# A gated delta rule's query decayed on GpSimd, its output summed in PSUM, and another scheduler model

## The chip, the cores and the metric

The kernel runs on one core of one Trainium2 chip. A core has TensorE (PE, matmuls; PEld is its weight load), VectorE (DVE), ScalarE (ACT), GpSimd (POOL) and a queue that issues DMAs (SP). The time is device microseconds of one launch, as the median over runs. A profiled execution gives a span (first to last instruction) and its own time, which is a little longer.

## The reference, cut to what matters

A decoder trunk of two layers over 1024 tokens of width 1024, all in float32. Layer 0 (even) is a dilated attention and an HGRN2 recurrence side by side, layer 1 (odd) a gated delta rule. Each layer is a projection in, the mixer, a projection out. The change touches the odd layer's recurrence, and the order of instructions everywhere.

```python
# per head, in chunks; q and k normalized, g the summed log decay inside a chunk
attn_qk = einsum('bhnid,bhnjd->bhnij', qc, kc) * decay
q_dec = qc * exp(gcum)[..., None]
k_tail = kc * exp(gcum[..., -1:] - gcum)[..., None]
def step(state, inp):
    v_new = u_n - einsum('bhcd,bhdv->bhcv', w_n, state)
    o = einsum('bhcd,bhdv->bhcv', qd_n, state) + einsum('bhij,bhjv->bhiv', a_n, v_new)
    new_state = state * gl_n + einsum('bhcd,bhcv->bhdv', kt_n, v_new)
```

There are 8 key heads and 16 value heads; two value heads share a key head's q and k and differ in their decays. The output o has two parts: what the state gives to the decayed q, and what the chunk's own values give.

## The kernel before

Matmuls of the projections run as three fp32r products of a high and a low part each (`mm3`, L151 to L153), 512 columns wide. Weights are cut into these parts by ACT (L116) and DVE (L117), one unit ahead.

The odd layer works on pairs: one key head and its two value heads, hh = 0 to 7, in chunks of 128 tokens (NT = 8). Three kinds of work are interleaved:

- `proj(j)` first runs `way_out(j - 2)` (two gate projections oz and the output of a finished pair), then four projections with a short convolution: k of pair j + 1 (tile kT), two halves v of pair j, q of pair j. `conv` runs one projection as two halves of 512 tokens. ACT copies a half from its PSUM bank into a staging tile (tag ub, one buffer; the profile calls its tiles uk, uv, uq after the projection); only then the target tile is asked for (`k_tile`, `q_tile`, `v_tile`), written by ACT (L902), and three DVE operations (L904), a Tanh (L907) and one more DVE operation (L908) finish it. Projections have two PSUM banks (tag "pj").
- `invert(hh)` builds the lower triangular matrices of a pair from kT (kk, L1063), inverts them in 32x32 blocks on DVE (L1084, L1086), and joins the blocks with small matmuls (qp, up, q, u) through bank "c". Its result U lies in the tile L.
- `recur(hh)` walks the eight chunks. For each: ks = kT'S (L1182), r (L1185, DVE), qs = q'S (L1188) with the two scalings oq (L1191, ACT), vp = U r (L1197), vt (L1200, DVE) and vn (L1202, ACT), kv (L1206), the new state S (L1210, DVE), op = A vn (L1217), the sum of op and oq into bv (L1220, DVE), squares for the norm (L1225, ACT). A for the next chunk comes from `attend`: qk (L1168) times the decay tile gca, which is read by DMA from gcd, added to a mask on POOL (L1156) and put through Exp on ACT (L1158).

PSUM has tags with a number of banks each: "pj" 2, "a" 2, "b" 2, "c" 1, "d" 1. Before, ks, kv and op take "b" in turn, and qs, vp and qk share the one bank "d".

The loop over pairs mixes the three: while recur(hh) runs, the fill is proj(hh + 1) blended with invert(hh + 1). Each generator yields rough amounts of PE time, and `mix` and `blend` lay as much fill between two steps as the yielded need says; in the last pair the output projection `out_last` is fill too.

```python
fill = proj(hh + 1) if hh < 7 else seq(way_out(6), gate7(), out_last(range(3), ["pj"]))
if hh < 7:
    fill = blend(invert(hh + 1), fill, 0.8)
mix(recur(hh), fill, 2.8)
drain(fill)
```

This makes an order of emission. The framework then lays out each engine's instructions: going through a simulated run of the program, it takes on every engine the first in the order of emission that is ready in that simulation, and it gives a tile a buffer of its tag when one is free (a buffer comes free when all who read or write its tile are done). In the attention of layer 0 the order of PE (for its last pair also that of DVE) is fixed as emitted (`manual_schedule`); everywhere else the simulation decides. What an engine runs on the chip is that fixed order, each instruction waiting for its semaphores.

A tag's buffers: kT 3, q 2, kn 3, L 2, bv 2, gca 2, ub 1. At the end, `y_parts(0)` of the odd layer takes two kT buffers and two kn buffers for the first tile of the output projection's input.

Of the kernel before, what the change touches and what calls it, by code (L numbers as in the profile page):

```python
# [82 lines left out]
def trunk_kernel(ctx: ExitStack, tc: tile.TileContext, x, ew, ewo, ow, owab, owo, nw, fnw, lbl, hnw,  # L83
# [11 lines left out]
    def bank(tag, shape, name):  # L95
        return pp.tile(shape, F32, name=name, tag=tag, bufs=BANKS[tag])
# [720 lines left out]
    def odd_layer(es):  # L817
# [107 lines left out]
        def k_tile(j):  # L925
            KT[j] = sp.tile([P, T], F32, name=f"kT{j}", tag="kT", bufs=3)
            return KT[j]
# [116 lines left out]
        def invert(hh):  # L1044
# [14 lines left out]
            for h in range(2):  # L1059
# [4 lines left out]
                for c in range(4 * h, 4 * h + 4):  # L1064
# [3 lines left out]
                    for e in range(2):  # L1068
                        dve.scalar_tensor_tensor(L[:, 2 * c + e, :], kk[:, c - 4 * h, :], SC[hh][:, 0, c, e:e + 1],
                                                 gcB[:, e, :], op0=ALU.mult, op1=ALU.mult)  # L1070
                yield (15 if h else 7.0), 0.9

# [36 lines left out]
            dve.tensor_copy(Q_[a0[1], :, 0:32], qp[a0[1]])  # L1109
            yield 1.5, 1.3  # L1110
            up = bank("c", [P, 16, 32], f"up{hh}")
# [12 lines left out]

            yield 2.0, 1.8
            for h in range(2):
# [22 lines left out]
        def recur(hh):  # L1149
# [4 lines left out]
            def decay_a(c):  # L1154
                DA = decays(hh, c, "a")
                pool.tensor_tensor(DA, DA, MA[:, None, :].to_broadcast([P, 2, 128]), op=ALU.add)  # L1156
                for e in range(2):
                    act.activation(DA[:, e, :], DA[:, e, :], AF.Exp, bias=gt["ngc"][:, c, 2 * hh + e:2 * hh + e + 1])  # L1158
                return DA

            def attend(c):

                DA = ahead_a.pop()
                if c < NT - 1:
                    ahead_a.append(decay_a(c + 1))
                qk = bank("d", [P, 128], f"qk{hh}_{c}")
                s = slice(c * 128, (c + 1) * 128)
                pe.matmul(qk, kT[:, s], q[:, s], start=True, stop=True)  # L1168
                A = sp.tile([P, 2, 128], F32, name=f"A{hh}_{c}", tag="A", bufs=2)
                dve.tensor_tensor(A, qk[:, None, :].to_broadcast([P, 2, 128]), DA, op=ALU.mult)  # L1170
                return A

            ahead_a = [decay_a(0)]
            yield 1.0
            A = attend(0)
            St = None
            for c in range(NT):
                col = [slice(2 * hh + e, 2 * hh + e + 1) for e in range(2)]
                s = slice(c * 128, (c + 1) * 128)
                if c:  # L1180
# [3 lines left out]
                    for e in range(2):  # L1184
                        dve.scalar_tensor_tensor(r_[:, e, :], ks[:, e, :], SC[hh][:, 1, c, e:e + 1],  # L1185
                                                 bv[:, c, e, :], op0=ALU.mult, op1=ALU.add)
                    qs = bank("d", [P, 2, 128], f"qs{hh}_{c}")
                    pe.matmul(qs, q[:, s], St, start=True, stop=True)  # L1188
                    oq = sp.tile([P, 2, 128], F32, name=f"oq{hh}_{c}", tag="oq")
                    for e in range(2):  # L1190
                        act.activation(oq[:, e, :], qs[:, e, :], AF.Copy, scale=gt["eg"][:, c, col[e]])  # L1191
                else:
                    r_ = bv[:, 0]
                yield 1.0
                vp = bank("d", [P, 2, 128], f"vp{hh}_{c}")
                for e in range(2):
# [7 lines left out]
                if c < NT - 1:  # L1204
# [9 lines left out]
                    St = Sn  # L1214
                op = bank("b", [P, 2, 128], f"op{hh}_{c}")
                for e in range(2):
                    pe.matmul(op[:, e, :], A[:, e, :], vn[:, e, :], start=True, stop=True)  # L1217
                A = attend(c + 1) if c < NT - 1 else None
                if c:
                    dve.tensor_tensor(bv[:, c], op, oq, op=ALU.add)  # L1220
                else:
                    dve.tensor_copy(bv[:, c], op)
                for e in range(2):
# [11 lines left out]
        def y_parts(g):  # L1235
            if g:
                return *y_tile(f"lo{g % 2}", 8 + g), g * 256
            yh = [sp.tile([P, T], F32R, name=f"oyh{c}", tag="kT", bufs=3) for c in range(2)]
            yl = [sp.tile([P, T], F32R, name=f"oyl{c}", tag="kn", bufs=3) for c in range(2)]
# [109 lines left out]
```

## Time and profile before

| | |
|---|---|
| median of 3 runs | 2271.49 us (2265.71 to 2271.65) |
| profiled execution | 2270.35 us, span 2268.6 us |
| mean granted TensorE clock | 0.992 |
| PE, PEld busy | 2162.0 us (95%), 1760.6 us (78%) |
| DVE, ACT, POOL busy | 1409.7 us (62%), 950.0 us (42%), 239.5 us (11%) |
| DMA | 184.15 MB, mean 81 GB/s |

How to read what follows: the busy slices are tenths of 40 equal parts of the span. A group's row has its line, engine, operation, tiles (out<-in) and shapes, then busy us and mean ns of one, then the engine's idle time just before these and what ended most of it. A row of one tile has the durations' least, middle and largest in ns and the first and the last start in us. A row of the timeline begins with the start and the duration in us. Waits have total us, times and the longest. PE's records of matmuls overlap, so the distance between starts says what one costs.

### The profile page before, as it was taken

What the parts mean: (1) busy time and instruction counts of PE and PEld (TensorE: products, weight loads), DVE (VectorE), ACT (ScalarE), POOL (GpSimd) and SP (SyncE); (2) the same over time, 40 slices, a digit from 0 to 9 for tenths busy, and PEclk for the clock granted to TensorE, in tenths of its full rate; (3) what the DMA queues carried; (4) which work ended last, traced back from release to release, by engine and by line L of the source; (5) the groups of instructions that cost most, each with busy time, mean ns of one, the idle gap of its engine ahead of it and who ended that gap; (6) DMA issues with size and microseconds to landing.
All of it is one profiled execution on the core that took longest, in us unless ns stands there. A gap on an engine that the chain in (4) does not pass through costs nothing. (4 is left out here: it accounts for less than half of the span.)

```text
span 2268.6 us, 52553 instructions
## 1 busy us (share of the span) xinstructions
PE 2162.0 (95%) x21781; PEld 1760.6 (78%) x21781; DVE 1409.7 (62%) x3236; ACT 950.0 (42%) x2551; POOL 239.5 (11%) x252
## 2 busy tenths in 40 slices
PE   7999999999999999989999988989898999899998
PEld 6888888898877878767886776767777777678787
DVE  6353535453444344457776986968878787755767
ACT  5233333333232232222237664655555555544223
POOL 0010101010000000000000013121212121210000
PEclk9999999999999999989999999999999999999999
DMA  4111111114342334353233222121212122124233
GB/s 146 38 48 48 43 49 47 48 34 126 91 128 71 109 91 122 97 162 108 93 116 104 61 55 67 51 78 41 77 51 76 49 71 65 58 64 153 85 112 112
DMA packets 100079, 184.15 MB, mean 81 GB/s; under 512 B 12672, under 2 KB 30208, under 8 KB 99840
## 3 DMA queue, kind: packets, MB, share of 16 engines
q1 hardware_dynamic: 99840, 180.79, 25.9%
q8 instruction: 171, 2.80, 0.5%
q14 instruction: 68, 0.56, 0.1%
HBM read 151.25 MB, written 29.49 MB: 80 GB/s over the span
## 5 line engine op out<-in xcount | busy, mean ns | idle before, releaser
L117 DVE TENSOR_TENSOR w_lo<-raww,w_hi 128x512 fp32r<-128x512 f32 x292 | 210.2, 722 | 199.5 <-ACT w_hi L116 196.8
L116 ACT CAST w_hi<-raww 128x512 fp32r<-128x512 f32 x292 | 181.1, 620 | 298.0 <-DMA raww<-in_ewo_dram 51.0
L647 ACT ACTIVATE P<-P,nm 128x256 f32<-128x256 f32 (+7 forms) x128 | 71.4, 559 | 133.9 <-DVE nm L645 133.9
L151 PE MATMUL op<-w_hi,yplo 128*128 128x512 f32 x288 | 113.7, 395 | 3.3 <-DVE hr L296 1.7
L153 PE MATMUL op<-w_hi,yplo 128*128 128x512 f32 x288 | 112.2, 390 | 0.0
L152 PE MATMUL op<-w_lo,yplo 128*128 128x512 f32 x288 | 112.2, 390 | 0.0
L151 PE MATMUL oz<-hn_hi,w_hi 128*128 128x512 f32 x256 | 109.9, 429 | 0.0
L151 PE MATMUL pv<-hn_hi,w_hi 128*128 128x512 f32 x256 | 106.7, 417 | 0.5 <-ACT uv L899 0.5
L296 DVE TENSOR_TENSOR hr<-hr,op 128x512 f32<-128x512 f32 x128 | 85.9, 684 | 34.2 <-PE op L153 33.6
L153 PE MATMUL pv<-hn_hi,w_lo 128*128 128x512 f32 x256 | 104.1, 407 | 0.0
L152 PE MATMUL oz<-hn_lo,w_hi 128*128 128x512 f32 x256 | 103.0, 402 | 0.0
L153 PE MATMUL oz<-hn_hi,w_lo 128*128 128x512 f32 x256 | 102.5, 400 | 0.0
L152 PE MATMUL pv<-hn_lo,w_hi 128*128 128x512 f32 x256 | 102.2, 399 | 0.0
L653 DVE STREAM_TRANSPOSE PB<-P 128x256 f32<-128x256 f32 (+3 forms) x64 | 54.6, 853 | 72.8 <-ACT P L647 72.8
L1156 POOL TENSOR_TENSOR gca<-gca,MA 128x256 f32<-128x256 f32 x64 | 50.6, 791 | 453.8 <-DMA gca<-gcd 252.8
L296 DVE TENSOR_TENSOR hres<-hres,op 128x512 f32<-128x512 f32 x96 | 64.7, 682 | 31.8 <-PE op L153 29.4
L642 DVE CUSTOM_DVE_ANT_0 P<-S,G 128x256 f32<-128x256 f32 (+7 forms) x128 | 58.2, 492 | 36.8 <-PE S L638 35.2
L904 DVE SCALAR_TENSOR_TENSOR vT<-uv,cws,vT 128x512 f32<-128x512 f32 x96 | 74.3, 774 | 4.7 <-ACT vT L902 3.8
L1084 DVE TENSOR_TENSOR tm<-Lp,Tp 128x126 f32<-128x126 f32 (+22 forms) x248 | 74.9, 302 | 3.7
L1158 ACT ACTIVATE gca<-gca,g_ngc 128x128 f32<-128x128 f32 x128 | 45.8, 401 | 69.3 <-POOL gca L1156 69.1
L151 PE MATMUL avp<-w_hi,hn_hi 128*128 128x256 f32 x256 | 74.5, 291 | 0.0
L151 PE MATMUL op<-w_hi,yphi 128*128 128x512 f32 x160 | 65.9, 412 | 8.5 <-ACT yphi L116 4.6
(367 smaller groups left out, 6292.1 us busy)
## 6 DMA issues: line engine op xcount, KB each, us to landing
raww<-in_ew_dram SPq DMA_DIRECT2D x128, 256.0 KB, 3.0
raww<-in_ow_dram SPq DMA_DIRECT2D x100, 256.0 KB, 3.0
V<-vd SPq DMA_DIRECT2D x64, 256.0 KB, 5.3
rawy<-ymix SPq DMA_DIRECT2D x64, 256.0 KB, 2.7
raww<-in_ewo_dram SPq DMA_DIRECT2D x32, 256.0 KB, 3.0
gcl<-gcd SPq DMA_DIRECT2D x64, 128.0 KB, 3.0
gca<-gcd SPq DMA_DIRECT2D x64, 128.0 KB, 3.0
ymix<-oy SPq DMA_DIRECT2D x32, 256.0 KB, 2.0
```

The costliest lines, as they stand in the source:

```text
L116: act.copy(hi, raw)
L117: dve.tensor_tensor(lo, raw, hi.bitcast(F32), op=ALU.subtract)
L151: pe.matmul(ps, lh, rh, start=start, stop=False)
L152: pe.matmul(ps, lh, rl, start=False, stop=False)
L153: pe.matmul(ps, ll, rh, start=False, stop=stop)
L296: dve.tensor_tensor(dst[:, n], src[:, n], ps, op=ALU.add)
L642: dve.tensor_tensor_reduce(Pm[:, e, w0:], S[e][:, w0:WG], G[:, w0:], 1.0, -3e38, op0=ALU.add, op1=ALU.max, accum_out=mx[:, e:e + 1])
L647: act.activation(Pm[:, e, w0:], Pm[:, e, w0:], AF.Exp, bias=nmx[:, e:e + 1], scale=0.125, accum_out=den[:, i, e:e + 1])
L653: dve.transpose(PB[:, :, i * WG + w0:(i + 1) * WG], Pm[:, :, w0:])
L904: dve.scalar_tensor_tensor(a[0][:, s], ub[:, i + s.start:i + s.stop], cws[:, tile_no, i:i + 1], a[0][:, s], op0=ALU.mult, op1=ALU.add)
L1084: dve.tensor_tensor(tm[:, :31 - k, :n], Lp[:, k, k + 1:, None].to_broadcast([P, 31 - k, n]), Tp[:, k:k + 1, :n].to_broadcast([P, 31 - k, n ...
L1156: pool.tensor_tensor(DA, DA, MA[:, None, :].to_broadcast([P, 2, 128]), op=ALU.add)
```

## The change

It does five things.

- The framework's simulation, by which each engine's order is fixed, becomes its detailed timeline (`schedule_with_timeline_sim=True`).
- q is decayed before the product instead of after: for each chunk but the first, Exp of the raw decays (ACT) gives qe, and POOL multiplies it with q, for both value heads. The product with the state becomes two 128x128 matmuls into the output's bank op, and A vn is added to them there. oq and the addition L1220 go; ACT copies op to bv.
- Banks: op alone in "d"; qk and vp move to "b", with ks and kv.
- kT has two buffers instead of three; the output's first tile takes one kT and one q buffer.
- Three distances in `invert` grow: 7.0 to 9.0, 1.5 to 3.0, 2.0 to 4.0.

```diff
         def k_tile(j):
-            KT[j] = sp.tile([P, T], F32, name=f"kT{j}", tag="kT", bufs=3)
+            KT[j] = sp.tile([P, T], F32, name=f"kT{j}", tag="kT", bufs=2)
...
-                yield (15 if h else 7.0), 0.9
+                yield (15 if h else 9.0), 0.9
...
-            yield 1.5, 1.3
+            yield 3.0, 1.3
...
-            yield 2.0, 1.8
+            yield 4.0, 1.8
...
             def decay_a(c):
                 DA = decays(hh, c, "a")
+                if c:
+
+                    qe = QE[c] = sp.tile([P, 2, 128], F32, name=f"qe{hh}_{c}", tag="qe", bufs=2)
+                    act.activation(qe, DA, AF.Exp)
+                    pool.tensor_tensor(qe, qe, q[:, None, c * 128:(c + 1) * 128].to_broadcast([P, 2, 128]), op=ALU.mult)
                 pool.tensor_tensor(DA, DA, MA[:, None, :].to_broadcast([P, 2, 128]), op=ALU.add)
...
-                qk = bank("d", [P, 128], f"qk{hh}_{c}")
+                qk = bank("b", [P, 128], f"qk{hh}_{c}")
...
-                    qs = bank("d", [P, 2, 128], f"qs{hh}_{c}")
-                    pe.matmul(qs, q[:, s], St, start=True, stop=True)
-                    oq = sp.tile([P, 2, 128], F32, name=f"oq{hh}_{c}", tag="oq")
+
+                    op = bank("d", [P, 2, 128], f"op{hh}_{c}")
+                    qe = QE.pop(c)
                     for e in range(2):
-                        act.activation(oq[:, e, :], qs[:, e, :], AF.Copy, scale=gt["eg"][:, c, col[e]])
+                        pe.matmul(op[:, e, :], qe[:, e, :], St[:, e, :], start=e == 0, stop=False, skip_group_check=True)
...
-                vp = bank("d", [P, 2, 128], f"vp{hh}_{c}")
+                vp = bank("b", [P, 2, 128], f"vp{hh}_{c}")
...
-                op = bank("b", [P, 2, 128], f"op{hh}_{c}")
+                if not c:
+                    op = bank("d", [P, 2, 128], f"op{hh}_{c}")
                 for e in range(2):
-                    pe.matmul(op[:, e, :], A[:, e, :], vn[:, e, :], start=True, stop=True)
+                    pe.matmul(op[:, e, :], A[:, e, :], vn[:, e, :], start=not c and e == 0, stop=True, skip_group_check=True)
...
-                if c:
-                    dve.tensor_tensor(bv[:, c], op, oq, op=ALU.add)
-                else:
-                    dve.tensor_copy(bv[:, c], op)
+                act.copy(bv[:, c], op)
...
-            yh = [sp.tile([P, T], F32R, name=f"oyh{c}", tag="kT", bufs=3) for c in range(2)]
+            yh = [sp.tile([P, T], F32R, name=f"oyh{c}", tag=t, bufs=2) for c, t in enumerate(("kT", "q"))]
...
-    with tile.TileContext(nc) as tc:
+    with tile.TileContext(nc, schedule_with_timeline_sim=True) as tc:
```

More of the change, by code (lines that the diff above doesn't have):

```diff
@@ L1171, in attend @@
                 return A
+            QE = {}
             ahead_a = [decay_a(0)]
```

## The prediction

> **What bounds the kernel now.** I read the page first, then a table of stretches cut where each value-head pair's recurrence begins, then who PE waited for inside them, then single tiles and rows of one pair.
>
> ```profile
> span 2268.6 us, 52553 instructions
> PE 2162.0 (95%) x21781; PEld 1760.6 (78%) x21781; DVE 1409.7 (62%) x3236; ACT 950.0 (42%) x2551; POOL 239.5 (11%) x252
> PE   7999999999999999989999988989898999899998
> ```
>
> PE is busy for 95% of the span, so 106.6 us is the most that any better order could give back. The digits below 9 lie at both ends, in slice 18 (the change from layer 0 to its output), and from slice 24 on: the odd layer, the only place that the diff's edits to the arithmetic touch.
>
> ```profile
> core 0: us, PE busy (x) PEld busy (x) DVE busy (x) ACT busy (x) POOL busy (x), PEclk, DMA share, GB/s
> 1276.40:1370.00 93.60, 85.86 (x627) 68.77 (x626) 81.81 (x231) 55.06 (x168) 11.09 (x15) 1.00 0.20 54
> 1370.00:1478.40 108.40, 97.94 (x821) 77.41 (x820) 88.11 (x251) 61.00 (x186) 26.25 (x30) 0.95 0.19 56
> 1592.80:1700.80 108.00, 99.96 (x700) 80.84 (x699) 85.48 (x225) 60.87 (x182) 21.57 (x24) 1.00 0.21 62
> sum 740.60, PE 678.17 PEld 545.29 DVE 591.88 ACT 414.30 POOL 143.33; mean PE 96.88 PEld 77.90 DVE 84.55 ACT 59.19 POOL 20.48
> ```
>
> These are pairs 0, 1 and 3 of seven, and the seven's sum: 740.6 - 678.2 = 62.4 us of idle PE. DVE is at 80%, ACT at 56%, POOL at 19%. PE sets the time, DVE is the engine nearest to joining it.
>
> ```profile
> PE op L1217 <- ACT vn L1202: 11.0, 14, 1.6
> PE ks L1182 <- DVE S L1210: 9.7, 7, 1.8
> PE vp L1197 <- ACT oq L1191: 7.2, 10, 1.6
> PE kk L1063 <- DVE L L1069: 5.7, 4, 1.5
> PE up L1114 <- DVE Q L1109: 4.6, 5, 1.5
> PE q L1130 <- ACT L L1118: 4.6, 5, 2.5
> ```
>
> The largest waits inside those 740.6 us (total, times, longest): the first three are steps of the recurrence, the last three of the inversion. All are short; nothing here is one big hole.
>
> **The arithmetic.** In each of 56 chunks the query product qs goes, with its two ACT scalings (oq) and the DVE addition L1220; added are an Exp of 128x256 on ACT, a multiplication on POOL, two 128x128 matmuls into the output's own bank, and an ACT copy of the bank (in all 64 chunks).
>
> ```profile
> L1191 ACT ACTIVATE oq<-qs,g_eg 128x128 f32<-128x128 f32 x110 | 34.0, 357 | 5.7 <-PE qs L1188 5.4
> L1202 ACT COPY vn<-vp 128x256 f32<-128x256 f32 x63 | 23.0, 365 | 22.4 <-DVE vt L1200 18.7 <-PE vp L1197 2.2 <-DVE uq L895 1.1
> L1055 ACT ACTIVATE gcl<-gcl 128x256 f32<-128x256 f32 x54 | 22.1, 410 | 0.5
> L1220 DVE TENSOR_TENSOR bv<-op,oq 128x256 f32<-128x256 f32 x55 | 22.9, 416 | 1.1 <-PE op L1217 1.1
> L1156 POOL TENSOR_TENSOR gca<-gca,MA 128x256 f32<-128x256 f32 x62 | 49.2, 793 | 446.3 <-DMA gca<-gcd 245.4 <-ACT jtq L920 40.0 <-DVE Tp L1086 36.2
> ```
>
> ACT loses 112 x 0.357 = 40.0 us and gains 56 x 0.410 + 64 x 0.365 = 46.3: +6, hidden in an engine that is 44% idle. DVE loses 56 x 0.416 = 23.3, and eight small copies of chunk 0. POOL gains 56 x 0.79 = 44 us, hidden, since it idles 446 us before L1156 alone; even at a chunk every 6.7 us (shown below) its two operations, 1.6 us, and the ACT passes around them fit. No DMA is added; SP's issues stay the same.
>
> ```profile
> 1665.03 0.61 PE L1217 MATMUL op<-vn,A 128*128 128x128 f32 x4
> 1665.48 0.39 PE L1168 MATMUL qk<-q,kT 128*128 128x128 f32 x2
> 1668.02 0.39 PE L152 MATMUL pv<-hn_lo,w_hi 128*128 128x512 f32 x1
> 1668.25 0.39 PE L153 MATMUL pv<-hn_hi,w_lo 128*128 128x512 f32 x1
> 1668.47 0.59 PE L1182 MATMUL ks<-S,kT 128*128 128x256 f32 x2
> 1668.90 0.59 PE L1188 MATMUL qs<-S,q 128*128 128x256 f32 x2
> ```
>
> PE starts are the honest measure: a pair of 128x128 products holds it 1665.48 - 1665.03 = 0.45, a 128x256 product 1668.90 - 1668.47 = 0.43, a projection matmul 0.23. So PE pays 56 x 0.02 = **+1 us**.
>
> **Banks.** qs shared bank "d" with vp, so vp waited for both scalings; vp now alternates with ks, kv and qk in "b". The 7.2 us go; taken whole, **-7** (0 to -7). New waits: the first half of op stands on PE ahead of vp and waits for POOL's qe and for the bank's copy of the chunk before. Nearest row: op on vn, 11.0 us. Both inputs are made about a chunk ahead, so I take 0 (0 to +11).
>
> **Wider distances.** More projection between the inversion's steps attacks 5.7 + 4.6 + 4.6 = 14.9 us; I take half, **-8** (0 to -15).
>
> **POOL against DVE.**
>
> ```profile
> 1633.06 0.88 POOL L1156 TENSOR_TENSOR gca<-gca,MA 128x256 f32<-128x256 f32 x1 [4.08 <-DMA gca<-gcd]
> 1633.38 0.71 DVE L1084 TENSOR_TENSOR tm<-Lp,Tp 128x130 f32<-128x130 f32 x1
> 1634.13 0.29 DVE L1086 TENSOR_TENSOR Tp<-Tp,tm 128x130 f32<-128x130 f32 x1
> ```
>
> While POOL adds, a DVE operation of the same width takes 0.71 instead of 0.29. At 0.42 for each new multiplication that is up to 56 x 0.42 = 24 us of DVE, as much as the removed addition gave it: DVE ends where it was (bounds -23 and +1), so no credit on the path. The Trainium skill, SBUF — State Buffer, "Who interferes with whom", says that a VectorE operation with two SBUF inputs and a GpSimd one that reads SBUF exclude each other for the whole instruction. The row agrees; by that rule the lengthening may reach the full 0.79 us, 44 us on DVE.
>
> **Two kT buffers, not three.** This is the largest term. While recur(hh) reads kT of pair hh, invert(hh+1) needs kT of hh+1, and proj(hh+1) writes kT of hh+2. With two slots that write must wait until recur(hh) has read its own kT for the last time, in ks of chunk 7. Pair 3:
>
> ```profile
> L902 ACT ACTIVATE kT<-uk,cws x2: 734/758/783, 1640.7 to 1647.0; 128x512 f32<-128x512 f32 x2
> L904 DVE SCALAR_TENSOR_TENSOR kT<-uk,cws,kT x6: 743/748/982, 1642.1 to 1652.1; 128x512 f32<-128x512 f32 x6
> L908 DVE SCALAR_TENSOR_TENSOR kT<-uk,kT x2: 667/680/692, 1646.6 to 1653.6; 128x512 f32<-128x512 f32 x2
> L1182 PE MATMUL ks<-S,kT x14: 377/379/454, 1606.2 to 1681.6; 128*128 128x256 f32 x14
> L899 ACT COPY uv<-pv x4: 576/583/588, 1658.4 to 1686.0; 128x512 f32<-128x512 f32 x4
> 1629.53 0.67 PE L1182 MATMUL ks<-S,kT 128*128 128x256 f32 x2 [1.79 <-DVE S L1210]
> 1636.21 0.59 PE L1182 MATMUL ks<-S,kT 128*128 128x256 f32 x2
> ```
>
> kT is written from 1640.7 to 1654.3; the last ks is at 1681.6. What is held behind that write? ACT and DVE can be given other work first. But the convolution's staging tile (tag ub) has one buffer: v0 can't be copied into it before kT is finished, and v0's two halves then hold both projection banks. PE can still run k's second half and both of v0, to 1668.5, where it stands at ks of chunk 6; after that it has no projection to run. From there: one chunk to ks(7) at the shortest spacing shown (1636.21 - 1629.53 = 6.7), 0.6 for ks, then the write: at least 0.76 + 6 x 0.748 + 2 x 0.68 + 0.6 = 7.2, today 13.6 among other work; I take 9, since less competes. Then v0's copy, 0.58. Sum 16.9 us without projections. PE still has two chunks of recurrence (19 passes of about 0.22 = 4.2), the transposes of k (0.9) and the next kk (1.8): 6.9. New idle 10.0, of which 16.9 x 8.0/108 = 1.3 is idle today: 8.7 a pair (7 with the shortest write, 13 with today's). Pairs 1 to 5: **+43** (15 if the recurrence gains a chunk on the projections, to 65).
>
> ```profile
> L904 DVE SCALAR_TENSOR_TENSOR kT<-uk,cws,kT x6: 743/744/746, 1283.0 to 1290.0; 128x512 f32<-128x512 f32 x6
> L1182 PE MATMUL ks<-S,kT x14: 377/379/454, 1321.9 to 1366.5; 128*128 128x256 f32 x14
> ```
>
> Pair 0 has no gates ahead of k: the write moves from 1283 to after the last ks, at best 1321.9 + 6 x 6.7 = 1362. The four halves of v1 and q (96 x 0.23 = 22 us), which now run before 1370, come after it. PE was idle 7.7 us there and can't make that up: **+20** (10 to 28). Pairs 6 and 7 write no third kT; the output's first y tile goes to a free q slot, 0.
>
> **The scheduler's timeline.** It may reorder every engine except where an order is fixed by hand. What remains to win in the seven stretches is 62.4 - 7.2 - 14.9 = 40 us; I take 45%, **-18** (-40 to +15: a PE that is full in layer 0 can only lose there).
>
> **Sum.** +1 - 7 - 8 + 43 + 20 - 18 = +31 on the profiled execution's 2270.35 (span 2268.6 and 1.75 around it): 2301. The median of the runs, 2271.49, is 1.1 higher: **2302**.
>
> **Rivals.** (1) The recurrence runs ahead and the slot is free in time: faster. It decides from where ks(7) ends about 9 us before 1658.4, v0's first copy, so 32 us earlier than now. For it: a chunk can take 6.7 us and is given 12.6 (1606.2 to 1681.6 in six). Against: PE always has a projection ready that stands earlier in the program, and takes it. Then no stall, -32: 2239. (2) The recurrence comes forward half as far, the stall halves to 32 and cancels the gains: 2271. (3) Idle PE also loses its clock:
>
> ```profile
> PEclk9999999999999999989999999999999999999999
> ```
>
> Slice 18 is where the clock slips; pair 1, with the most idle PE of its stretch (10.5 us), has 0.95 of it above, 0.05 x 108.4 = 5.4 us. Six such pairs add 32: 2334. The Trainium skill, TensorE: Matmul & The Clock Gate, "The HAM clock gate", has the rate halved after an idle window of about 3.4 us; pair 1 agrees in kind. (4) Each new POOL multiplication holds up a DVE operation of the chain for its whole 0.79 us: 44 - 23 = 21 us, 2323; for it the 0.71, against it that few of the chain's operations read SBUF twice. It is the SBUF page's rule at its worst.
>
> **How the numbers follow.** Stall as summed 0.42 (own range 2280 to 2335); rival 1 0.34; 2 0.10; 3 0.09; 4 0.05. Three runs of this kernel spread by 0.26%, so about 0.3% (6.8 us) can be told from no change. Faster 0.34, same 0.10, slower 0.56. The range, 2230 to 2345, leaves out the end of rival 1 with a better order and that of rival 3 with the longer write.
>
> **What would show it.** Right: kT's first write behind the last ks of the pair before; PE idle 8 to 13 us between v0's and v1's projections of each pair; vp no longer waiting for ACT. Wrong: kT written well before the projections of v0 end, or the inversion's and recurrence's waits on PE down by more than 60 us.

## The result and the profile after

| | before | after |
|---|---|---|
| median | 2270.68 us (2265.71 to 2271.65, 4 runs) | 2422.97 us (2420.24 to 2425.95, 4 runs) |
| profiled execution | 2270.35 us, span 2268.6 | 2421.64 us, span 2419.9 |
| mean granted TensorE clock | 0.992 | 0.957 |

The changed kernel is slower: ratio 1.0676, 95% interval 1.0655 to 1.0697. The page of the changed kernel, its first lines:

```profile
span 2419.9 us, 52729 instructions
PE 2239.2 (93%) x21893; PEld 1829.4 (76%) x21893; DVE 1416.0 (59%) x3172; ACT 953.1 (39%) x2557; POOL 281.2 (12%) x308
PE   7999999999999999899997688898989898999998
PEclk9999999999999999899999798999989797999999
```

PE lost share (95 to 93%) although its busy time rose by 77 us, with only 112 small matmuls more: a busy PE at half clock takes twice as long (a pair of ks records, 0.59 us in before, is 1.22 below, at 1768.55, where the clock is a half). The clock row shows it: eights and sevens from slice 23 on, where before has nines. The odd layer as a whole (from its first matmul to the last gate projection oz) went from 879.7 to 1012.0 us; it starts 14.4 us later (13.1 of that is there when layer 0's attention begins its products with V, L667, at 566.2 instead of 553.1), and the end takes 4.6 more.

Pairs 0, 1 and 3 of the odd layer, cut where each pair's first qk begins, with PE's clock:

```profile
core 0: us, PE busy (x) PEld busy (x) DVE busy (x) ACT busy (x) POOL busy (x), PEclk, DMA share, GB/s
1311.00:1432.00 121.00, 90.10 (x729) 73.29 (x730) 90.60 (x255) 53.50 (x169) 24.27 (x31) 0.80 0.15 40
1432.00:1561.00 129.00, 109.81 (x743) 86.57 (x734) 82.77 (x219) 63.02 (x186) 27.39 (x31) 0.89 0.19 52
1688.00:1815.00 127.00, 110.75 (x739) 90.87 (x738) 89.14 (x225) 65.10 (x195) 28.39 (x30) 0.95 0.22 57
```

Pair 3 (last row) takes 127 us where before it took 108.0; 16 us are idle in it instead of 8, and its clock has fallen from 1.00. The waits of PE in the odd layer of the changed kernel (total, times, longest):

```profile
PE op L1224 <- ACT vn L1208: 30.8, 24, 2.8
PE tk L917 <- DVE kT L908: 19.4, 5, 5.4
PE kv L1212 <- DVE vt L1206: 18.0, 28, 1.7
...
PE op L1197 <- ACT bv L1226: 7.7, 8, 2.4
```

The first was 11.0, the third 1.3, and the wait of vp on oq, 7.2, is gone as predicted. tk, the transposes of a kT that is written late, had waited 3.1. Pair 3, from the views of the tile kT and of PE's timeline:

```profile
L1188 PE MATMUL ks<-S,kT x16: 377/379/793, 1720.2 to 1844.1; 128*128 128x256 f32 x16
L904 DVE SCALAR_TENSOR_TENSOR kT<-uk,cws,kT x6: 737/743/743, 1770.8 to 1774.1; 128x512 f32<-128x512 f32 x6
L902 ACT ACTIVATE kT<-uk,cws x2: 707/714/722, 1769.8 to 1770.4; 128x512 f32<-128x512 f32 x2
...
1745.85 0.39 PE L153 MATMUL pv<-hn_hi,w_lo 128*128 128x512 f32 x1
1768.55 1.22 PE L1188 MATMUL ks<-S,kT 128*128 128x256 f32 x2
1778.44 1.12 PE L917 MATMUL tk<-ident,kT 128*128 128x128 f32 x4 [5.44 <-DVE kT L908]
1781.77 0.78 PE L151 MATMUL pv<-hn_hi,w_hi 128*128 128x512 f32 x1
```

The last projection matmul of v0 is at 1745.85. The pair's last ks comes 22.7 us later, at 1768.55; only then is kT written (from 1769.8), and v1 begins at 1781.77. For 35.9 us PE has no projection. It had been predicted at 16.9.

**A ledger.** From the trace's clock records and PE's busy time I worked out, for the odd layer of each kernel: its length, PE's idle time, and the part of PE's busy time that lies where the granted clock is a half. At half clock a matmul takes twice as long, so half of that part is lost time. "Sum" is the added idle time plus half of the added half-clock busy time; it stands beside the measured difference to before.

| kernel | odd layer us | idle | busy at half clock | difference | sum |
|---|---|---|---|---|---|
| before | 879.7 | 69.0 | 15.0 | | |
| after | 1012.0 | 133.3 | 137.0 | +132.3 | 64.3 + 61.0 = 125.3 |
| b_kt2 | 999.0 | 132.5 | 123.9 | +119.3 | 63.5 + 54.5 = 118.0 |
| b_tl | 958.1 | 96.1 | 120.9 | +78.4 | 27.1 + 53.0 = 80.1 |
| a_kt3 | 929.0 | 81.0 | 100.3 | +49.2 | 12.0 + 42.7 = 54.7 |
| a_notl | 986.2 | 140.2 | 71.1 | +106.5 | 71.1 + 28.1 = 99.2 |
| a_full3 | 903.9 | 88.0 | 20.2 | +24.2 | 18.9 + 2.6 = 21.5 |
| b_tl_nodma | 932.0 | 75.6 | 113.6 | +52.3 | 6.6 + 49.3 = 55.9 |
| b_nodma | 871.4 | 61.4 | 22.0 | -8.3 | -7.6 + 3.5 = -4.1 |
| b_m55 | 902.8 | 82.8 | 50.7 | +23.1 | 13.8 + 17.9 = 31.7 |

It closes within 9 us in these rows; in b_m19, b_kt2_m19, a_notl_m19, b_pe and b_tl_pe, described below, it misses by 9.5 to 15.3. So about half of what the change cost in the odd layer is idle time, and the other half is clock.

### The profile page after: what moved, and what is told of

It is laid out like the page before. It is cut to its first block, busy times and chain, and to the rows that moved or that the text cites. A ratio compares the mean times of both kernels' runs of the same rounds, so it can differ in the third digit from the quotient of the medians.

```text
span 2419.9 us, 52729 instructions
## 1 busy us (share of the span) xinstructions
PE 2239.2 (93%) x21893; PEld 1829.4 (76%) x21893; DVE 1416.0 (59%) x3172; ACT 953.1 (39%) x2557; POOL 281.2 (12%) x308
## 5 line engine op out<-in xcount | busy, mean ns | idle before, releaser
L116 ACT CAST w_hi<-raww 128x512 fp32r<-128x512 f32 x292 | 180.5, 620 | 337.9 <-DMA raww<-in_ewo_dram 51.7
L647 ACT ACTIVATE P<-P,nm 128x256 f32<-128x256 f32 (+7 forms) x128 | 71.4, 559 | 133.0 <-DVE nm L645 132.9
L151 PE MATMUL oz<-hn_hi,w_hi 128*128 128x512 f32 x256 | 104.8, 410 | 0.8 <-ACT uq L899 0.4
L1160 POOL TENSOR_TENSOR qe<-qe,q 128x256 f32<-128x256 f32 x56 | 43.7, 780 | 442.2 <-ACT qe L1159 303.7
L904 DVE SCALAR_TENSOR_TENSOR vT<-uv,cws,vT 128x512 f32<-128x512 f32 x96 | 84.1, 896 | 10.7 <-ACT vT L902 10.0
L1224 PE MATMUL op<-vn,A 128*128 128x128 f32 x256 | 49.3, 322 | 31.0 <-ACT vn L1208 30.8
L1086 DVE TENSOR_TENSOR Tp<-Tp,tm 128x126 f32<-128x126 f32 (+22 forms) x248 | 74.3, 300 | 5.4
L696 POOL TENSOR_TENSOR ay<-ay,sg 128x512 f32<-128x512 f32 x16 | 20.2, 1282 | 489.9 <-DMA ay<-rdd 362.1
L1224 PEld LDWEIGHTS op<-vn,A 128*128 128x128 f32 x256 | 42.2, 223 | 44.7 <-ACT vn L1208 41.7
```

What stands on the lines that cost most here:

```text
L116: act.copy(hi, raw)
L151: pe.matmul(ps, lh, rh, start=start, stop=False)
L647: act.activation(Pm[:, e, w0:], Pm[:, e, w0:], AF.Exp, bias=nmx[:, e:e + 1], scale=0.125, accum_out=den[:, i, e:e + 1])
L904: dve.scalar_tensor_tensor(a[0][:, s], ub[:, i + s.start:i + s.stop], cws[:, tile_no, i:i + 1], a[0][:, s], op0=ALU.mult, op1=ALU.add)
L1086: dve.tensor_tensor(Tp[:, k + 1:, :n], Tp[:, k + 1:, :n], tm[:, :31 - k, :n], op=ALU.subtract)
L1224: pe.matmul(op[:, e, :], A[:, e, :], vn[:, e, :], start=not c and e == 0, stop=True, skip_group_check=True)
```

## The experiments

Kernels whose name begins with a are the changed kernel with something undone, those with b the kernel before with something added. Ratios are to runs of the kernel before on the same chip; its median there was 2270.8 to 2276.5 us.

**1. The change taken apart.** Three buffers for kT again (a_kt3; for room qe has one buffer); two kT buffers alone (b_kt2); the timeline alone (b_tl); everything without the timeline (a_notl).

```diff
# a_kt3, against after (and y_parts for three)
-            KT[j] = sp.tile([P, T], F32, name=f"kT{j}", tag="kT", bufs=2)
+            KT[j] = sp.tile([P, T], F32, name=f"kT{j}", tag="kT", bufs=3)
...
-  name=f"qe{hh}_{c}", tag="qe", bufs=2)
+  name=f"qe{hh}_{c}", tag="qe", bufs=1)
# b_kt2, against before (and y_parts as in the change)
-            KT[j] = sp.tile([P, T], F32, name=f"kT{j}", tag="kT", bufs=3)
+            KT[j] = sp.tile([P, T], F32, name=f"kT{j}", tag="kT", bufs=2)
# b_tl, against before; a_notl is the reverse, against after
-    with tile.TileContext(nc) as tc:
+    with tile.TileContext(nc, schedule_with_timeline_sim=True) as tc:
```

> The changed kernel with three kT buffers again and, to make room, one qe buffer instead of two; all else as changed. Theory S (the write of the third kT waits for the recurrence, and projections stand still behind it): PE's gap between the projections of v0 and v1, 35.7 us in pair 3 of the changed kernel, closes, kT is written some 30 us earlier in the pair, and the time falls by 100 to 140 us, to 2283 to 2323. Theory T (the order made with the detailed timeline is itself worse, and the slot only shows where): it falls by less than 50 us and stays above 2370. Theory A (the new arithmetic and the banks lengthen the recurrence's step): it stays above 2370 too, with 16 to 19 us between the ks of early chunks.

> The kernel before with two kT buffers, and the output's first tile in one kT and one q buffer: this part of the change alone. Theory S in the size of the prediction: +63 us, near 2333 (2285 to 2365), with kT's first write in each pair behind the last ks and PE idle 8 to 13 us a pair between v0 and v1. Theory S in the size that the changed kernel's trace shows (v0 ends at chunk 4, not 6): +100 to +140. Theories T and A: less than +30.

> The kernel before with the detailed timeline in the scheduler, nothing else. The prediction had -18 (-40 to +15): 2253 (2231 to 2286). Theory T: +60 or more, above 2330, with longer distances between the ks of early chunks than the 12.6 us of before. Theory S: within 25 us of before.

> The changed kernel with the scheduler's simulation as before; two kT buffers stay. Theory S alone: still slow, 2330 or more, since the slot is as short. Theory T: near 2290 or below. Theory A: near 2400, as the arithmetic stays.

| kernel | median us | ratio |
|---|---|---|
| a_kt3 | 2343.98 | 1.0304 (1.0287 to 1.0321) |
| b_kt2 | 2396.57 | 1.0530 (1.0506 to 1.0554) |
| b_tl | 2369.64 | 1.0415 (1.0399 to 1.0430) |
| a_notl | 2375.22 | 1.0442 (1.0426 to 1.0457) |

Either part alone is harmful: +122 us for two kT buffers, which is theory S in the size of the changed kernel's trace, and +95 for the timeline, which is theory T's. a_notl, where the short slot stays, is as slow as theory S has it. a_kt3 lies between the two theories' numbers: with the buffer back, the timeline's harm stays. Together the parts do not add up to 217, the whole change costs 152; as I read it, because both leave the same recurrence without projections beside it. The stall of b_kt2's pair 3, in the timeline of PE:

```profile
1612.95 0.39 PE L153 MATMUL pv<-hn_hi,w_lo 128*128 128x512 f32 x1
1613.18 0.59 PE L1182 MATMUL ks<-S,kT 128*128 128x256 f32 x2
1616.81 0.71 PE L1197 MATMUL vp<-r,L 128*128 128x128 f32 x4 [2.60 <-ACT oq L1191]
1619.53 0.67 PE L1182 MATMUL ks<-S,kT 128*128 128x256 f32 x2
1627.46 1.11 PE L917 MATMUL tk<-ident,kT 128*128 128x128 f32 x4 [1.19 <-DVE kT L908]
1632.11 0.80 PE L151 MATMUL pv<-hn_hi,w_hi 128*128 128x512 f32 x1 [0.98 <-ACT uv L899]
```

This is the predicted stall step by step: v0 ends at ks of chunk 6 (1613.18), one chunk of 6.35 us to ks of chunk 7, then the write, then v1 at 1632.11. 18.9 us, predicted 16.9. Per pair (cut at each recurrence's first qk; length, PE idle, busy at half clock):

| pair | before | b_kt2 | b_kt2_m19 (below) | b_tl |
|---|---|---|---|---|
| 0 | 94.5, 7.7, 0 | 132.9, 24.9, 48.8 | 134.8, 25.1, 52.4 | 124.0, 21.9, 38.5 |
| 1 | 107.4, 10.5, 8.1 | 129.4, 21.3, 15.1 | 111.7, 9.9, 3.1 | 127.0, 9.9, 25.9 |
| 2 | 115.2, 9.8, 3.4 | 125.3, 18.2, 13.2 | 109.1, 8.6, 0 | 113.9, 10.9, 7.2 |
| 3 | 108.0, 8.0, 0 | 126.3, 16.8, 19.6 | 109.1, 7.4, 3.4 | 111.9, 8.3, 8.6 |
| 4 | 107.1, 7.3, 0 | 123.2, 16.8, 12.8 | 109.4, 8.0, 3.1 | 112.7, 10.1, 6.6 |
| 5 | 108.1, 8.1, 0 | 125.6, 18.3, 14.4 | 109.7, 8.8, 0 | 112.5, 8.8, 9.4 |

Pairs 1 to 5 of b_kt2 gained 47.7 us of idle time (predicted 43), pair 0 17.2 (predicted 20). In time they cost 84 and 38.

**2. Is the kT stall the late read?** My rival 1 had said from where it decides: ks of chunk 7 some 32 us earlier. The mixer's number that lays fill between two steps of the recurrence moves it there.

```diff
-            mix(recur(hh), fill, 2.8)
+            mix(recur(hh), fill, 1.9)
```

> Two kT buffers (2396.6 us), and the number by which the mixer lays fill between two steps of the recurrence lowered from 2.8 to 1.9, so that the recurrence comes forward by about 32 us in a pair: the point that my rival 1 named. On PE the last ks of pairs 1 to 5 then stands behind 114 projection matmuls of the pair instead of 144, where the kT slot is asked for. Theory S (the cost is the read of kT that comes after the projections have run out): the stall of pairs 1 to 5 is gone, pair 0's stays (20 to 28 us): 2285 to 2315. Theory K (two buffers cost otherwise, or the recurrence without cover costs as much): 2360 or more.

> Control: the kernel before with 1.9 for 2.8. The recurrence's chunks stand nearer to each other (11 to 30 projection matmuls between two, where before has 12 to 42), with a stretch of 174 behind the last. A chunk's chain takes at least 6.7 us, of which 24 matmuls cover 5.5: 2268 to 2300 under all theories.

> The change without its timeline (two kT buffers, arithmetic, banks, distances: 2375.2 us), with 1.9 for 2.8 in the mixer. On PE the last ks of pairs 1 to 5 moves from behind 144 projection matmuls of the pair to behind 96, in front of the end of v0. Theory S (the stall is the late read of kT, here too): as two kT buffers with 1.9 (2317.0), plus what arithmetic, banks and distances cost by themselves with three (12 to 21): 2320 to 2340. If arithmetic and banks gain under the tighter recurrence, as they did beside two buffers and 2.8 (-21): 2290 to 2300. Theory K (another cost of the smaller tag): above 2350.

b_kt2_m19 took 2316.95 us (ratio 1.0188, 1.0172 to 1.0203), the control b_m19 2288.63 (1.0067, 1.0052 to 1.0082), a_notl_m19 2339.67 (1.0304, 1.0286 to 1.0321). b_kt2_m19 is 2 us above theory S's interval, the control inside its own. Of the 122 us of two buffers 28 are left over the control, and the table above says where: in pair 0 (+40 against before, +37 against the control), where k's projection has no gates ahead of it and so asks for the slot at once; pairs 1 to 5 are 3 us longer in all than in before and 14 shorter than in the control. The same stretch as the stall above, in the windows of b_kt2 and then of b_kt2_m19:

```profile
1613.00:1632.00 19.00, 10.46 (x46) 7.85 (x44) 12.43 (x34) 10.62 (x42) 3.40 (x4) 0.76 0.10 28
```

```profile
1613.00:1632.00 19.00, 18.05 (x87) 15.14 (x88) 14.21 (x22) 8.10 (x14) 0.00 (x0) 1.00 0.12 37
```

PE is busy for 18.05 of 19 us at full clock instead of 10.46 at 0.76. The late read is the cause. It holds for the changed arithmetic too: a_notl_m19 is at the upper end of theory S's interval, 36 us below a_notl (31 by the ratios), and the stretches of 16 to 17 us without a projection that a_notl has in pairs 1 to 5 are gone.

**3. What does the half clock cost?** Matmuls whose result is not used were added to b_kt2, so that PE is less idle about the stall.

```diff
+            def keep(c, n):
+                if hh < 6 and c >= (6 if hh else 1):
+                    ps = bank("c", [P, 2, 128], f"dum{hh}_{c}_{n}")
+                    for _ in range(n):
+                        pe.matmul(ps, ident, kn[:, 0:2, :], start=True, stop=True)
...
+                keep(c, 2)
...
+                keep(c, 2 if c < NT - 1 else 16)
```

> The kernel before with two kT buffers (2396.6 us, 122 over before), and added to it matmuls that compute nothing that is used: two of 128 x 256 behind each step of the last two chunks of a pair's recurrence and sixteen at its end, so that TensorE has work in the stall at the head of a pair's second projection. Theory C (the clock: of the 122 us only 63 are idle time of PE in this layer, and the rest is that 136 us of the layer more run at half clock, which the idle time brings about): the half-clock time falls to less than half and the kernel gets faster though it has more to do, 2335 to 2360. Theory I (idle time and waits alone, and the half clock in the rows costs nothing that matters): the stall stays as long as it was and the added matmuls are in the way, 2395 to 2420.

2426.43 us (ratio 1.0664, 1.0634 to 1.0693): slower than b_kt2. Theory C's number was missed by 66 us, and theory I's lies nearer, though the half-clock time fell to about a half, which only C expected. The parts say more. The added matmuls' group:

```profile
L1177 PE MATMUL dum<-kn,ident 128*128 128x256 f32 x372 | 94.5, 386 | 0.5 <-ACT L L1118 0.2
```

PE got 94.5 us more work, and the odd layer only 31.9 more time (1030.9 us). Idle time fell from 132.5 to 112.2, busy time at half clock from 123.9 to 61.1: 20.3 and half of 62.8, together 51.7 us back. The records of overlapping matmuls make 94.5 an upper figure for the work, and with it the account closes within 11 us. The clock does come back when PE is fed, and by this account the time that it costs with it; feeding it this way costs more than it returns.

**4. What makes the timeline slow?** First its DMA waits: the decays' first step on ACT reads a tile that is in SBUF instead of the one that a DMA brings (this part of the computation gives another value), with the timeline and without.

```diff
-                gcB = decays(hh, c, "l")
+                gcB = sp.tile([P, 2, 128], F32, name=f"gcl{hh}_{c}", tag="gcl", bufs=2)
...
-                    act.activation(gcB[:, e, :], gcB[:, e, :], AF.Relu, bias=...)
+                    act.activation(gcB[:, e, :], MA, AF.Relu, bias=...)
```

> The kernel before with the timeline (2369.6 us, 95 over before), and the decays of the lower triangle (L1054) taken from a tile that lies in SBUF instead of the tile that a DMA brings, so that ACT does not wait for that DMA; what this part of the computation gives is thereby another value. Theory D (the timeline orders ACT's decays ahead of the recurrence's copies, and where their DMA is late ACT stands, and behind it PE's vp and op wait: 25.5 and 23.3 us in the layer against 7.2 and 11.0): at most 2330, at least 40 us of the 95 come back, beyond what the control gains. Theory L (the timeline puts the projections in coarse lumps, 363 changes between projections and other matmuls where before has 575, and the recurrence's chain is left without cover at a pair's start): 2355 to 2370, no more than the control gains.

> Control to the run above: the kernel before with the same edit to L1054 and the same part of the computation another value. ACT waits 34 times for these transfers here, 37.5 us in all, while TensorE is idle for 69 us of 880 in the layer: theories D and L both expect 2260 to 2272, a gain of 0 to 10.

b_tl_nodma took 2344.92 us (1.0300, 1.0285 to 1.0315), b_nodma 2260.44 (0.9930, 0.9915 to 0.9945). The timeline's kernel gained 25 us, the control 16, where both theories had 0 to 10 for it. Neither number of theory D or L was met, and without these transfers the timeline still costs 84 of its 95 us. PE's largest waits in the odd layer, of b_tl and then of b_tl_nodma:

```profile
PE vp L1197 <- ACT oq L1191: 25.5, 18, 3.7
PE op L1217 <- ACT vn L1202: 23.3, 15, 3.1
```

```profile
PE vp L1197 <- ACT oq L1191: 15.7, 13, 2.2
PE op L1217 <- ACT vn L1202: 9.2, 10, 2.9
```

The waits on ACT halved, and idle time fell from 96.1 to 75.6 us. But the control lost 7.6 us of idle time as well (69.0 to 61.4), so of the 27.1 us that the timeline adds, 14.2 stay. Busy time at half clock stayed too (120.9 to 113.6; the control has 22.0). So ACT behind late DMAs is about half of the idle part of the timeline's cost, and idle time is not the larger part. Where the clock falls, in the windows of b_tl:

```profile
1254.00:1372.00 118.00, 111.00 (x667) 90.68 (x666) 92.15 (x238) 63.61 (x166) 7.25 (x10) 0.97 0.22 58
1383.00:1441.00 58.00, 38.23 (x121) 25.13 (x119) 37.22 (x124) 25.91 (x91) 5.67 (x8) 0.62 0.14 34
1547.00:1590.00 43.00, 31.15 (x270) 24.45 (x271) 20.19 (x64) 21.77 (x74) 10.68 (x12) 0.74 0.19 43
```

From 1383 to 1441 PE runs chunks 1 to 7 of pair 0 without one projection matmul (the third row is the end of pair 1, where the last three chunks have none). PE's instruction order says why. The projection matmuls before each of the seven ks, counted through the layer:

```
pair 0  before 390 408 419 438 453 468 481     b_tl 504 504 504 504 504 504 504
pair 3  before 1056 1092 1111 1124 1164 1200 1242
        b_tl   1080 1080 1123 1186 1247 1294 1352
        b_kt2  1056 1092 1111 1124 1164 1200 1200
        after  1061 1109 1163 1200 1200 1200 1200
```

As I read the counts, the timeline takes each projection as soon as it is ready: they run ahead in lumps of 40 to 70 between two chunks, until the gates oz of a pair whose recurrence is not finished hold both projection banks (pair 0's oz begin at 1353, and the transposes that let them go come at 1448); then the recurrence runs bare. In the changed kernel the two parts meet: lumps of 48, 54 and 37 bring the projections to the place where kT's next write has to wait (1200) when ks of chunk 4 is next, two chunks sooner than in b_kt2. That is why the gap was 35.9 us and not 18.9; in a_notl, the changed kernel without the timeline, it is 17.1 (lines in experiment 5).

Next, PE's order in the loop over pairs fixed as emitted, with and without the timeline:

```diff
+        with tc.manual_schedule(engines={mybir.EngineType.PE}):
             for hh in range(8):
```

> The kernel before with the timeline (2369.6 us), and in the loop over pairs of the odd layer PE's order fixed as emitted, so that the timeline orders the other engines only. Theory L (the harm is PE's order: the timeline takes every projection as soon as it is ready, so they come in lumps and leave the head of each pair's recurrence to itself, idle and at half clock): what the odd layer lost, 78 us, comes back, layer 0's 14 and the end's 5 stay: 2285 to 2305. Theory D (the harm is in ACT's order, the decays ahead of the recurrence's copies): the order of ACT is still the timeline's, 2335 to 2370.

> Control to the run above: the kernel before without the timeline, PE's order in the loop over pairs of the odd layer fixed as emitted. Under L and D alike this says what a rigid order on PE costs or gains by itself: the simulation may now no longer fill a wait of PE with a later projection, but the order of emission is already an even mixture; 2265 to 2300.

2491.25 us (1.0958, 1.0938 to 1.0979) and 2424.68 (1.0660, 1.0644 to 1.0676), both far above everything expected: the control is no neutral ground. Of b_pe and then of b_tl_pe:

```profile
PE qp L1107 <- DVE Un L1090: 159.4, 8, 24.8
PE vp L1197 <- ACT oq L1191: 5.7, 8, 1.3
PE op L1217 <- ACT vn L1202: 3.2, 3, 1.8
```

```profile
PE vp L1197 <- ACT oq L1191: 26.1, 9, 5.0
PE op L1217 <- ACT vn L1202: 21.6, 9, 3.3
```

In emitted order PE stands eight times before the inversion's joins until DVE is through with the 32x32 blocks, 159.4 us (147.1 in b_tl_pe). What can be read is the difference of the two, 67 us, of which 45 lie in the odd layer, with the same order on PE in its loop over pairs: the waits on ACT rise from 8.9 to 47.7 us. The orders of the other engines are thus part of the timeline's cost. How much of it PE's order makes, these two do not tell.

Last, lumps without the timeline, by the mixer's number:

```diff
-            mix(recur(hh), fill, 2.8)
+            mix(recur(hh), fill, 5.5)
```

> The kernel before, without the timeline, with 5.5 for 2.8: on PE the projections come in lumps as the timeline places them (36, 78, 78 between the first chunks of a pair, then 12, 12 and 10; with the timeline 43, 63, 60 and none at the head). Theory L (lumps leave the recurrence's chain bare, and PE then also runs at half clock): idle up by 20 to 40, half-clock time over 80 us, 2320 to 2375. Theory D (the timeline's cost is ACT behind late DMAs, which this kernel does not have more of than before): 2270 to 2300.

2304.57 us (1.0135, 1.0120 to 1.0150), between the theories. The lumps are there (78, 78), but each later chunk keeps 10 to 12 projection matmuls, and that suffices. The later chunks of its pair 3:

```profile
1693.00:1713.00 20.00, 18.48 (x99) 14.56 (x98) 12.36 (x33) 9.45 (x30) 1.46 (x2) 1.00 0.14 40
```

Chunks of 6.2 us, PE busy for 18.48 of 20, full clock. The lumps are not free: by idle time and half of the half-clock time, with the cuts of the table above, pairs 2 to 5 lost 22.6 us more than in before, and in b_tl, with its lumps, 19.1. Pairs 0 and 1 tell the two apart: 7.3 us in b_m55, 41.8 in b_tl, where ten of their chunks are bare. What costs most is the chunk that is left with nothing.

**5. Arithmetic, banks and distances alone.** With three kT buffers and without the timeline: with one buffer for qe (a_kt3_notl), with two (a_full3; vt takes the place of r), and as the latter with the old distances (b_arith2).

```diff
# a_full3, against the changed kernel without timeline and with three kT buffers
-                    vt = sp.tile([P, 2, 128], F32, name=f"vt{hh}_{c}", tag="vt")
+                    vt = sp.tile([P, 2, 128], F32, name=f"vt{hh}_{c}", tag="r")
# b_arith2, besides
-                yield (15 if h else 9.0), 0.9
+                yield (15 if h else 7.0), 0.9
-            yield 3.0, 1.3
+            yield 1.5, 1.3
-            yield 4.0, 1.8
+            yield 2.0, 1.8
```

> The changed kernel without its timeline and with three kT buffers (to make room, q's exponentials of the decays have one buffer instead of two): arithmetic, banks and distances are what is left of the change. Theory R (the rest is a gain of its own, worth what it was worth beside the other parts: 2375.2 with two kT buffers against 2396.6 for two kT buffers alone, -21; 2344.0 with the timeline against 2369.6 for the timeline alone, -26): 2245 to 2255 us, 1% faster than before. Theory F (the rest only fills holes that the other two parts tear open, and before has no such holes): 2265 to 2280, no change. My prediction had -15 for these parts, 2256.

> The change without its timeline and with three kT buffers, and with both buffers of qe (to make room, vt takes the place of r, whose last reader it needs anyway): arithmetic, banks and distances in full. The run with one qe buffer gave 2286.5 us beside 2276.5 of before. Theory Q (the single qe buffer cost it: qe of the next chunk, on ACT's and POOL's order, waited for this chunk's product): 2245 to 2268. Theory F (arithmetic, banks and distances gain only where the two other parts have torn holes; alone they are no gain): 2276 to 2292.

> As the run above, but with the distances of before: arithmetic and banks alone. If the wider distances are worth the 8 us of my prediction, this is about 8 us slower than the run above; if they push the inversion's steps late and harm, it is faster by as much; if they do nothing, the two agree within 5 us.

2286.5 us (1.0045, 1.0028 to 1.0061), 2295.73 (1.0099, 1.0078 to 1.0120) and 2289.89 (1.0071, 1.0054 to 1.0087). None is a gain; a_kt3_notl and a_full3 are slower than theory F's intervals too, and b_arith2 is 5.8 us below a_full3 with intervals that overlap. The waits of PE in the odd layer of b_arith2:

```profile
PE op L1224 <- ACT vn L1208: 17.4, 22, 2.4
PE ks L1188 <- DVE S L1216: 9.5, 12, 1.0
PE vp L1203 <- DVE r L1191: 7.3, 5, 1.7
...
PE kv L1212 <- DVE vt L1206: 4.9, 5, 1.2
...
PE op L1197 <- ACT bv L1226: 2.8, 6, 0.7
```

The 7.2 us of vp behind oq are gone. In their place op on vn rose by 6.4, vp on r by 3.4 and kv on vt by 3.6, and the bank's copy on ACT adds 2.8: 16.2 us. Where these waits show depends on the rest: in a_kt3_notl, where vt keeps its own buffer and qe has one, the four rise by 0.7, 6.2, 9.3 and 1.9, 18.1 us. Beside the timeline or two kT buffers, where vp waited 24 to 26 us for oq, the same edits gained 21 to 26 us (a_notl against b_kt2, a_kt3 against b_tl). In a_notl the gain lies where PE has no projection. Pair 3:

```profile
1723.74 0.59 PE L1188 MATMUL ks<-S,kT 128*128 128x256 f32 x2
1728.20 0.60 PE L1188 MATMUL ks<-S,kT 128*128 128x256 f32 x2
1740.58 0.50 PE L151 MATMUL pv<-hn_hi,w_hi 128*128 128x512 f32 x1 [0.98 <-ACT uv L899]
```

A bare chunk takes 4.5 us where b_kt2's takes 6.35, and the stretches without projections in pairs 0 to 5 are 140 us together instead of 163.

**6. Two tries at ACT's DMA waits.** b_nodma had given 16 us by leaving the transfer out. b_gcl3 issues it a chunk earlier into a third buffer, with vt in r's place for room; b_spread takes the four products of a burst apart.

```diff
# b_gcl3 (bufs=3 and vt's tag not shown)
+            raw = [decays(hh, 0, "l")]
             def decay_l(c):
-                gcB = decays(hh, c, "l")
+                gcB = raw.pop()
+                if c < NT - 1:
+                    raw.append(decays(hh, c + 1, "l"))
# b_spread
+                    if c % 4 < 3:
+                        yield 1.3, 0.1
-                yield (15 if h else 7.0), 0.9
+                yield (11 if h else 4.0), 0.6
```

> The kernel before with a third buffer for the decays gcl and their DMA issued a chunk earlier (vt takes the place of r to make room); nothing else changes, and the order of projections and recurrence on PE is the same but for pairs 0 and 1. ACT waited 37.5 us for these transfers in the odd layer. Without any transfer the kernel took 2260.4 us beside 2276.5. If those waits hold up the recurrence's copies on ACT: 2258 to 2268; if it was the missing transfer's own traffic that gave the gain: 2270 to 2280.

> The kernel before with the inversion's eight products L taken apart: a step of its generator behind each chunk where four came in one burst, the distances between them in sum as before. PE's order is the same but for a few places. The four decay tiles of a burst share two buffers, so the third waits for the first's reader and then 2.9 us for its transfer. If that wait is what gave the 16 us: 2260 to 2270; if ACT's order is fixed by the simulation in the same places anyhow: 2272 to 2278.

b_gcl3 took 2288.79 us (1.0066, 1.0042 to 1.0091), outside both expectations. It did not do what it was for; ACT's wait in the odd layer, 37.5 us in before, became

```profile
ACT gcl L1057 <- DMA gcl<-gcd: 52.5, 31, 4.2
```

Its move of vt into r's place was not run alone, and stands in a_full3 and b_arith2 too, so up to 15 us of theirs may be that move; a_kt3_notl has none of it. b_spread is no change that counts (2272.78 us; 1.0014, 1.0005 to 1.0024): the decays gcl stand in its trace within a few places of where ACT's order had them. No kernel that computes the whole beat the kernel before.

## Why the prediction was wrong

It forecast 2302 us, in a range up to 2345. The direction, the place and the mechanism of the largest term were right; the time was 121 us over.

- **Two kT buffers, +63.** As idle time it came out as written: 63.5 us in b_kt2, 47.7 in pairs 1 to 5 and 17.2 in pair 0 (43 and 20 predicted; that the sum agrees to half a us is luck), and experiment 2 shows the mechanism. The term was mis-sized as time, since it put the clock at nothing: these stalls also take the clock, and b_kt2's half-clock busy time rose by 108.9 us, of which half, 54.5, is lost. The odd layer grew by 119, not 63.
- **Rival 3** named this, priced at 5.4 a pair, +32 in all, with a chance of 0.09. It was no rival but a part of the first term. Its price per pair was read from pair 1 of before (not the one with the most idle PE, as it said: that is pair 6, 11.0 us at 0.98); in pairs 1 to 5 of b_kt2 the half-clock loss averages 6.4 us, and in pair 0, which was priced like the others, 24.4. Not all idle time takes the clock: a_full3 has 18.9 us more of it, in waits of at most 3.0 us with projections around them, and lost 2.6 to the clock.
- **The scheduler's timeline, -18 (-40 to +15).** The step that failed: "what remains to win in the seven stretches is 40 us; I take 45%". An idle time that exists says nothing of whether another order will recover it. Alone the timeline cost 95 us; of the profiled span's 100, 16 lie ahead of the odd layer, 5 at the end and 78 in it. Shown: longer waits on ACT (13 us of idle time by the DMAs, over the control), and bare chunks at half clock, with 38.5 and 25.9 us of busy time at it in pairs 0 and 1.
- **Additivity.** The sum treated the timeline and the kT slot as separate. They meet in one gap, which in pair 3 is 35.9 us instead of 16.9. In all they cost less together than apart, 152 us against 217.
- **Banks, -7.** The wait went as said; the new waits, taken as 0 with a bound of +11, were 16 us in b_arith2 and 18 in a_kt3_notl.
- **Distances, -8.** a_full3 is 5.8 us above b_arith2: no gain, and rather a loss, though the intervals overlap. Of the waits that they were to shorten one did, kk on L, 6.8 us without them and 2.0 with them; up on Q went from 4.8 to 7.7 and q on L from 4.1 to 5.4, so the three are 15.7 and 15.1 us in all.
- **The arithmetic, +1, and POOL against DVE, no credit.** Both stand: the two halves of op hold PE for four records 0.11 us apart in b_arith2, 0.44 beside qs's 0.43, DVE's busy time is 1416.0 us against 1409.7, and POOL's new operation measured 0.780 us against 0.79 taken:

```profile
L1160 POOL TENSOR_TENSOR qe<-qe,q 128x256 f32<-128x256 f32 x56 | 43.7, 780 | 442.2 <-ACT qe L1159 303.7 <-DVE q L908 114.1 <-DVE r L1191 12.4
```

- **Rivals 1 and 2** did not happen: no recurrence ran ahead by itself. Moved ahead by the mixer's number, it did remove the stall. **Rival 4**, POOL's lock, did not happen in the chain: its DVE operations have the middle durations of before (r 343 ns, S 342 and 341, vt 424 and 419), and idle time and clock make up 125 of the 132 us. What is longer beside POOL in the changed kernel is other operations, so L904, 1.11 us in the mean where a POOL operation overlaps it and 0.75 where none does.

Open: how the timeline's 78 us in the odd layer divide between PE's order and ACT's (b_tl_pe had no neutral control), why layer 0's attention begins 13 us later (not tried), and whether vt in r's place costs anything.

## What to carry to other kernels

A stall of TensorE that leaves a stretch thin is to be priced twice: as idle time, and as the work beside and behind it at half clock; here the second was nearly as large as the first (54.5 and 63.5 us in b_kt2), while short waits between projections cost almost no clock (2.6 us in a_full3). Before a buffer is taken from a tile, compare where its last reader stands in the engine's order with where the next writer asks for it, and move the reader forward first if it is late. A scheduler's order is judged by the stretches in which the chain is left without cover, not by the idle time that is there to win: ten to twelve cheap matmuls beside each step were enough in pair 3 of b_m55, none were not in b_tl.

## What the runs showed of the hardware

The half clock did not need a long gap. In b_tl it was granted from 1396.7 to 1430.8, 34.1 us on end. In the 3.4 us before the clock fell PE was busy for 1.40 us, and its longest gap there was 1.98. A gap of 3.33 us opened as the clock fell, and after it the only one over 0.8 us was of 1.48. The window of these us:

```profile
1397.00:1431.00 34.00, 23.82 (x64) 14.85 (x64) 24.18 (x80) 16.25 (x58) 2.90 (x4) 0.50 0.11 28
```

PE was busy for 70% of it by records that are twice as long because of the clock; at full clock the same work would have filled about a third. It came back for 3.4 us at 1430.8 and fell again, so a thinly used PE stays slow. The Trainium skill, TensorE: Matmul & The Clock Gate, "HAM oscillation — how this bites in real kernels", puts the rule as no idle gap of PE above about 3.4 us, and has half of the throttled time as the loss. The second agrees with the ledger, which takes half of the busy part of that time. The first is too mild for these rows: 123.9 us of b_kt2's busy time were at half clock with a single gap over 3.4 us in its odd layer (5.2 us, at 1362). Over the 20 us of b_m55 in which PE was busy for 18.48, the clock stayed whole; what share of use lies between is not shown here.
